# A later release for the first attention units of each head group in a two-layer hybrid decoder

## The chip, the cores and the metric

The kernel runs on one core of one Trainium2 chip. The metric is the device time of one execution in microseconds (us). Before the change it is 1654.51 us, the median of three runs that lie between 1652.82 and 1655.21 us. The engines are called PE (TensorE, with PEld for its weight loads), DVE (VectorE), ACT (ScalarE), POOL (GpSimd) and SP (SyncE, which issues every transfer of this kernel).

## The reference

The input is x, 1024 tokens by 1024 channels. Two decoder layers follow each other. In each one a token mixer is applied, then x becomes LayerNorm(alpha * x + mixer(x)), then a sigmoid gate adds a projected per-layer embedding. The mixer of the first layer, the one that matters here, is dilated sliding-window attention in three groups, (window 128, stride 1), (512, 4) and (2048, 16), with 16 heads of 64 channels each:

```python
for gi, (window, dil) in enumerate(A_GROUPS):
    q, k, v = split_cols(h[..., base:base + 3 * A_WIDTH], [A_WIDTH] * 3)   # h = x @ w_in
    q, k = apply_rope(q), apply_rope(k)
    o, lse = banded_attention(strided(q), strided(k), strided(v), window // dil)
    outs.append(o); lses.append(lse)
wts = softmax(stack(lses), axis=0)
o = einsum('gbsh,gbshd->bshd', wts, stack(outs))
return (o * silu(z)) @ w_out
```

The second layer is sliding-window attention with grouped queries and a sink logit per head.

## The kernel before, in words

Tokens are handled in 8 tiles of 128. Weights come in blocks of 1024 rows by 512 columns. A block is loaded in four pieces (`Block.load`, L102, `wraw<-in_wa_dram`), its largest entry is found on DVE (`maxima`, L109, then L226 to L230, a small matmul at L237 and L239), and it is split into a high and a low fp16 part (`split`, L132 on ACT and L133 on DVE, four pieces each). These steps form one long list, of which each projection tile draws a few (`prepare`). A raw buffer is loaded anew once its block is split, and a block is split into its slot once the block before in that slot is `released`.

A projection tile (`lin`, L272 to L274) is 24 matmuls of 512 columns on PE. The first layer (`layer_a`) goes through two halves of the heads (`pair`), each through the dilation groups 1, 2 and 0, so there are six rounds. A round has three blocks of 8 tiles, 24 tiles in all: a value block, then two query-and-key blocks (`i` = 0 and 1, four heads each, together eight heads). Two blocks of the gate z come behind the six rounds.

Behind a value tile `v_out` splits it into `vh` (L368, ACT) and `vl` (L369, DVE). Behind a query-and-key tile `rope_out` turns it: two DVE products (L347, L350), a POOL sum (L351), the high part on ACT (L357), the low part on POOL (L358), a swapped copy on ACT (L361), and one transposing transfer `qk<-hl` from SP (L362). The tile `qk` has 8 buffers.

The attention of one token tile and four heads is a unit. `score` (L385 on PE, 8 matmuls or 16 where two key tiles are seen) reads `qk`; DVE adds the mask and takes the maximum (L389, four times); ACT makes the bias (L393), four exponentials (L395) and the high part `phl` (L399); POOL, or DVE for every fourth tile, makes the low part (L401); SP transposes it to `pT` (L404). `value` (L416 to L418, 12 or 24 matmuls) multiplies by `vh` and `vl`; ACT writes it out (L695) and SP stores it (`scr<-st`, L704). In dilation group 0 the second unit of a token tile (odd `q`) hands a `merge` to a list: it loads the three dilation groups' outputs (`gt<-scr`, L752, two buffers), weighs them on DVE, ACT and POOL (L758 to L784) and stores them (`oa<-gt`, L788).

The order on PE is planned with a counter. `lin` calls `sub_tick` after the third and the sixth of its eight steps (9 and 18 matmuls), and `progress` calls it at the tile's end, so time goes in thirds of a tile:

```python
    def later(self, w, fn):
        self.due.append([self.work_done + w - 0.01, fn])

    def sub_tick(self):
        self.work_done += self.tile_w / 3.0
        ready = [e for e in self.due if e[0] <= self.work_done]
        ...
        self.credit = min(self.credit + self.upt * self.tile_w / 3.0, 2.0)
        if self.credit >= 0.999:
            self.credit -= 1.0
            self.unit_step()
```

`unit_a` is called when two thirds of its tile are counted, and asks with `later(UNIT_LAG, ...)`, UNIT_LAG = 1.67, that its unit be put at the end of the queue `self.units`. `unit_step` takes the next unit off that queue in order, runs the `value` of the unit that was taken three steps earlier, and then the `score` of the new one. `upt` is the number of steps for one tile: 0.75 in the six rounds (a step in every fourth third), 1.0 in the last block of the last round, and 2.0 from the z blocks on.

The program so written is then put in order for each engine by a scheduler that follows a modelled timeline: an instruction that the model does not see as ready is passed by later ones that are. On the chip each engine then keeps to that order.

Behind the rounds `mixed` multiplies the attention output by the gate, applies the output projection (blocks `wo`, whose memory the attention buffers held before) and normalises.

Of the kernel before, what the change touches and what calls it, by code (L numbers as in the profile page):

```python
# [78 lines left out]
UNIT_LAG = 1.67  # L79
# [60 lines left out]
class Trunk:  # L140
# [544 lines left out]
    def unit_a(self, q, g, n, qk, vh, vl, cs, ncs, cv, scr):  # L685
        nc, at = self.nc, self.att
        tiles = [n] if g == 2 or (n % 2 == 0 if g == 1 else n == 0) else [n - 1, n]
        mask = self.mask_2 if g == 2 else self.mask_a[:, (2 - len(tiles)) * P:]

        def stats():  # L690
            st = at.tile([P, 4 * HD + 8], F32, tag="st", name="st", bufs=len(self.pipe) + 1)
            return st, st[:, 4 * HD:4 * HD + 4], st[:, 4 * HD + 4:]

        def outp(o, st):
            nc.scalar.activation(st[:, 0:4 * HD], o.rearrange("p h c -> p (h c)"), AF.Copy, scale=cv)  # L695
            d = scr[q // 2][g][:, q % 2, :]
            if g == 1:
                b = 512 * (n % 2) + n // 2
                d = d[b:b + 509:4]
            elif g == 2:  # L700
                d = d[n:n + 1017:8]
            else:
                d = d[n * P:(n + 1) * P]
            nc.sync.dma_start(d, st)  # L704
            if g == 0 and q % 2:
                self.merges.append(self.merge(n, q // 2, scr[q // 2]))

        kas = [lambda h, sw, t=qk[i]: t[:, 4 + 4 * sw + h, :] for i in tiles]
        self.later(UNIT_LAG, lambda: self.unit(lambda h: qk[n][:, h, :], kas, mask, cs, ncs,
                                          lambda h, kb: vh[:, tiles[kb], h, :], lambda h, kb: vl[:, tiles[kb], h, :],  # L710
                                          stats, outp, n % 4 != 0))

# [452 lines left out]
```

## Time and profile before

| | us |
|---|---|
| median of three runs | 1654.51 |
| the profiled execution's own time | 1658.58 |
| its span, first to last instruction | 1656.8 |
| PE busy | 1584.4 (96% of the span) |
| DVE busy | 1084.4 (65%) |
| ACT busy | 922.7 (56%) |
| POOL busy | 660.2 (40%) |

The profile is of one execution, which took 4.07 us more than the median. Its mean granted TensorE clock is 0.987 of full speed. In a row of the timeline the first number is the start in us from the span's start and the second the duration; a bracket at the end gives the engine's idle time just before and what ended it. Rows that start with an engine and a line and hold "<-" are waits: total us, number, longest.

### The profile page before, as it was taken

The numbers are of one execution on the slowest core, as the hardware profiler recorded it, in microseconds if no ns is written. First come the engines' busy times: TensorE is split into PE (matmuls) and PEld (weight loads), VectorE is DVE, ScalarE is ACT, GpSimd is POOL, SyncE is SP. The second block draws the span as 40 slices with busy tenths as digits, with TensorE's granted clock in tenths as the row PEclk, the third lists the DMA queues.
The fourth block names the chain that finished last, engine by engine and source line by source line (L and its number), as shares of the span: only waits on it lengthen the run. The fifth ranks groups of instructions, "written<-read, shape, count | busy, mean of one in ns | idle before, by whom it ended". The sixth has DMA issues, their size and how long they took to land. (4 is left out here: it accounts for less than half of the span.)

```text
span 1656.8 us, 29015 instructions
## 1 busy us (share of the span) xinstructions
PE 1584.4 (96%) x10579; PEld 880.8 (53%) x10579; DVE 1084.4 (65%) x2619; ACT 922.7 (56%) x2050; POOL 660.2 (40%) x477
## 2 busy tenths in 40 slices
PE   8999999999999999989999987889999998999998
PEld 3455676655556556656545543334455555544444
DVE  6766655655666777656566657877356988778731
ACT  4537765674776576556657833533334888754321
POOL 0015624432553576345235652452323552225331
PEclk9999999999999999999999998999999999999999
DMA  9618766774886788557558986989975898998963
GB/s 362 251 61 172 174 143 139 152 166 106 167 162 177 188 208 190 153 127 167 139 130 187 194 229 212 334 208 264 242 189 107 163 204 166 197 300 212 261 197 109
DMA packets 543792, 311.02 MB, mean 188 GB/s; under 512 B 473120, under 2 KB 494240, under 8 KB 543392
## 3 DMA queue, kind: packets, MB, share of 16 engines
q1 hardware_dynamic: 543648, 309.16, 75.3%
q8 instruction: 83, 1.36, 0.3%
q14 instruction: 61, 0.50, 0.1%
HBM read 137.78 MB, written 54.92 MB: 116 GB/s over the span
## 5 line engine op out<-in xcount | busy, mean ns | idle before, releaser
L272 PE MATMUL lin<-whl,xhl 128*128 128x512 f16 x1280 | 488.6, 382 | 0.4 <-ACT zu L719 0.4
L273 PE MATMUL lin<-whl,xhl 128*128 128x512 f16 x1280 | 488.0, 381 | 0.0
L274 PE MATMUL lin<-whl,xhl 128*128 128x512 f16 x1280 | 487.7, 381 | 0.0
L351 POOL TENSOR_TENSOR t<-t,t 128x512 f32<-128x512 f32 (+1 forms) x120 | 153.9, 1282 | 303.5 <-DVE t L350 290.3
L401 POOL TENSOR_TENSOR phl<-sm,phl 128x1024 f16<-128x1024 f32 (+1 forms) x88 | 156.1, 1774 | 231.6 <-ACT phl L399 189.3
L109 DVE TENSOR_REDUCE wpm<-wraw 128x1 f32<-128x1024 f32 (+1 forms) x132 | 157.0, 1198 | 98.3 <-DMA wraw<-in_wa_dram 57.6
L274 PEld LDWEIGHTS <-xhl 128*128 128x128 f16 x1280 | 149.3, 117 | 127.7 <-issue 3.5
L272 PEld LDWEIGHTS <-xhl 128*128 128x128 f16 x1280 | 149.3, 117 | 120.1 <-issue 3.9
L273 PEld LDWEIGHTS <-xhl 128*128 128x128 f16 x1280 | 149.6, 117 | 116.7 <-issue 3.4
L395 ACT ACTIVATE sm<-sm,st,cs 128x128 f32<-128x128 f32 (+1 forms) x384 | 203.6, 532 | 3.4
L358 POOL TENSOR_TENSOR hl<-t,hl 128x512 f16<-128x512 f32 (+1 forms) x120 | 144.7, 1206 | 130.4 <-ACT hl L357 130.4
L389 DVE CUSTOM_DVE_ANT_0 sm<-s,tab 128x256 f32<-128x256 f32 (+1 forms) x512 | 157.2, 358 | 31.3 <-PE s L385 26.3
L133 DVE SCALAR_TENSOR_TENSOR whl<-wraw,s,whl 128x1024 f16<-128x1024 f32 (+1 forms) x116 | 167.3, 1492 | 10.0 <-ACT whl L132 9.9
L357 ACT ACTIVATE hl<-t 128x512 f16<-128x512 f32 (+1 forms) x120 | 72.3, 602 | 133.2 <-POOL t L351 131.4
L347 DVE TENSOR_TENSOR t<-lin,rope 128x512 f32<-128x512 f32 (+1 forms) x120 | 78.9, 657 | 77.6 <-PE lin L274 53.3
L132 ACT ACTIVATE whl<-wraw,s 128x1024 f16<-128x1024 f32 (+1 forms) x116 | 121.8, 1122 | 5.1 <-DVE s L212 5.0
L272 PE MATMUL lin<-whl,x2T 128*128 128x512 f16 (+1 forms) x320 | 114.5, 358 | 0.0
L274 PE MATMUL lin<-whl,x2T 128*128 128x512 f16 (+1 forms) x320 | 114.5, 358 | 0.0
L273 PE MATMUL lin<-whl,x2T 128*128 128x512 f16 (+1 forms) x320 | 114.5, 358 | 0.0
L399 ACT ACTIVATE phl<-sm 128x1024 f16<-128x1024 f32 (+1 forms) x128 | 110.2, 861 | 1.2
L385 PE MATMUL s<-qk 128*128 128x128 f16 x1120 | 81.7, 221 | 11.8 <-DMA qk<-hl 11.8
L361 ACT ACTIVATE hl<-hl 128x512 f16<-128x512 f16 (+1 forms) x104 | 63.2, 608 | 53.5 <-POOL hl L358 53.3
(187 smaller groups left out, 2880.9 us busy)
## 6 DMA issues: line engine op xcount, KB each, us to landing
wraw<-in_wa_dram SPq DMA_DIRECT2D x56, 512.0 KB, 5.6
scr<-st SPq DMA_DIRECT2D x96, 132.0 KB, 2.3
gt<-scr SPq DMA_DIRECT2D x48, 264.0 KB, 3.4
wraw<-in_wav_dram SPq DMA_DIRECT2D x24, 512.0 KB, 6.2
prh<-pro SPq DMA_DIRECT2D x32, 256.0 KB, 4.0
wraw<-in_wg_dram SPq DMA_DIRECT2D x16, 512.0 KB, 9.1
wraw<-in_wb_dram SPq DMA_DIRECT2D x16, 512.0 KB, 6.5
xg<-y SPq DMA_DIRECT2D x16, 512.0 KB, 3.7
```

Of the source, the lines that this page charges most:

```text
L109: k.nc.vector.tensor_reduce(pm[:, c:c + 1], self.raw[:, c * q:(c + 1) * q], axis=AX.X, op=ALU.max, apply_absolute_value=True)
L132: nc.scalar.activation(hl[:, 0, sl], self.raw[:, sl], AF.Copy, scale=self.s)
L133: self.last = nc.vector.scalar_tensor_tensor(hl[:, 1, sl], self.raw[:, sl], self.s, hl[:, 0, sl], op0=ALU.mult, op1=ALU.subtract)
L272: mm(ps, xh(kt), wh, start=(kt == 0), stop=False)
L273: mm(ps, xh(kt), wl, start=False, stop=False)
L274: mm(ps, xl(kt), wh, start=False, stop=(kt == NK - 1))
L351: self.at_pool = nc.gpsimd.tensor_add(t1[:, :nh * HD], t1[:, :nh * HD], t2[:, :nh * HD])
L358: nc.gpsimd.tensor_sub(hl[:, :nh, HD:P], rv, hl[:, :nh, 0:HD])
L389: nc.vector.tensor_tensor_reduce(sm[:, h, :nk], ps[:, i, :nk], mask, 1.0, -3e38, ALU.add, ALU.max, mx[:, h:h + 1])
L395: nc.scalar.activation(sm[:, h, :nk], sm[:, h, :nk], AF.Exp, bias=nbias[:, h:h + 1], scale=cs, accum_out=sums[:, h:h + 1])
L399: nc.scalar.activation(hl[:, 0], sm[:, :, :nk], AF.Copy)
L401: eng.tensor_sub(hl[:, 1], sm[:, :, :nk], hl[:, 0])
```

## The change

One line is added in `unit_a`, and the lag that is handed to `later` is no longer the constant. For even `q` (the block with `i` = 0 of each round) the lag of token tile n is 1.67 + max(0, 0.67 - n/3): 2.34 for n = 0, 2.00 for n = 1, and 1.67 as before from n = 2 on. For odd `q` it is 1.67 as before.

```diff
@@ -706,7 +706,8 @@
         kas = [lambda h, sw, t=qk[i]: t[:, 4 + 4 * sw + h, :] for i in tiles]
-        self.later(UNIT_LAG, lambda: self.unit(lambda h: qk[n][:, h, :], kas, mask, cs, ncs,
+        lag = UNIT_LAG + (max(0.0, 0.67 - n / 3.0) if q % 2 == 0 else 0.0)
+        self.later(lag, lambda: self.unit(lambda h: qk[n][:, h, :], kas, mask, cs, ncs,
                                           lambda h, kb: vh[:, tiles[kb], h, :], lambda h, kb: vl[:, tiles[kb], h, :],
                                           stats, outp, n % 4 != 0))
```

## Rows read from the trace of the kernel before

**Rows 1.** The page: the span and PE's share.
```profile
span 1656.8 us, 29015 instructions
PE 1584.4 (96%) x10579; PEld 880.8 (53%) x10579; DVE 1084.4 (65%) x2619; ACT 922.7 (56%) x2050; POOL 660.2 (40%) x477
```
**Rows 2.** Waits of PE, whole span: us in total, times, longest us.
```profile
PE s L237 <- DVE mdd L230: 18.7, 3, 8.0
PE s L385 <- DMA qk<-hl: 11.8, 4, 5.2
```
**Rows 3.** Timeline of PE around the first scores of rounds 2 to 5.
```profile
265.81 0.62 PE L385 MATMUL s<-qk 128*128 128x128 f16 x8 [2.46 <-DMA qk<-hl]
...
402.81 0.19 PE L416 MATMUL o<-vh,pT 128*128 128x64 f16 x1
...
407.26 0.61 PE L385 MATMUL s<-qk 128*128 128x128 f16 x8
...
550.86 0.19 PE L416 MATMUL o<-vh,pT 128*128 128x64 f16 x1
...
551.56 0.39 PE L272 MATMUL lin<-whl,xhl 128*128 128x512 f16 x1
...
554.59 0.38 PE L274 MATMUL lin<-whl,xhl 128*128 128x512 f16 x1
...
557.69 1.03 PE L385 MATMUL s<-qk 128*128 128x128 f16 x8 [2.72 <-DMA qk<-hl]
...
708.92 1.03 PE L385 MATMUL s<-qk 128*128 128x128 f16 x8 [5.18 <-DMA qk<-hl]
```
**Rows 4.** Windows behind two of them: us, busy by engine, granted PE clock, DMA.
```profile
557.69:561.00 3.31, 3.31 (x15) 1.80 (x16) 2.12 (x10) 1.17 (x3) 1.27 (x1) 0.53 1.10 357
708.92:714.50 5.58, 5.58 (x20) 2.72 (x21) 3.49 (x14) 3.58 (x11) 1.29 (x2) 0.51 0.55 134
```
**Rows 5.** Timelines of DVE, POOL and SP ahead of the 708.92 score.
```profile
693.39 5.38 DVE L133 SCALAR_TENSOR_TENSOR whl<-wraw,s,whl 128x1024 f16<-128x1024 f32 x4 [0.35 <-ACT whl L132]
698.70 0.68 DVE L347 TENSOR_TENSOR t<-lin,rope 128x512 f32<-128x512 f32 x1
...
700.05 1.28 POOL L351 TENSOR_TENSOR t<-t,t 128x512 f32<-128x512 f32 x1 [5.94 <-DVE t L350]
...
698.80 1.76 SPq L102 DMA_DIRECT2D wraw<-in_wa_dram  x4
...
703.92 2.10 SPq L362 DMA_TRANSPOSE qk<-hl  x1
```
**Rows 6.** Timelines of DVE, ACT, POOL: the round's last unit before.
```profile
686.13 0.41 DVE L389 CUSTOM_DVE_ANT_0 sm<-s,tab 128x256 f32<-128x256 f32 x1
...
687.62 0.30 ACT L393 ACTIVATE st<-mx,ncs 128x4 f32<-128x4 f32 x1 [1.25 <-DVE mx L389]
...
690.77 1.06 ACT L399 ACTIVATE phl<-sm 128x1024 f16<-128x1024 f32 x1
...
691.96 2.15 POOL L401 TENSOR_TENSOR phl<-sm,phl 128x1024 f16<-128x1024 f32 x1 [4.71 <-issue]
```
**Rows 7.** Windows ahead of the first turned tile: us, PE, PEld, DVE, ACT, POOL.
```profile
687.50:700.05 12.55, 12.55 (x90) 8.68 (x89) 9.22 (x17) 9.18 (x17) 2.15 (x1) 1.00 0.44 109
535.20:546.88 11.68, 11.68 (x97) 6.82 (x96) 10.72 (x15) 7.22 (x11) 2.25 (x3) 1.00 0.35 86
```
**Rows 8.** The layer's end: DVE's timeline, then waits of 987 to 1060 us.
```profile
938.65 0.18 DVE L758 TENSOR_REDUCE mM<-gt 128x8 f32<-128x24 f32 x1 [2.91 <-DMA gt<-scr]
...
940.34 5.77 DVE L133 SCALAR_TENSOR_TENSOR whl<-wraw,s,whl 128x1024 f16<-128x1024 f32 x4
946.02 0.17 DVE L768 TENSOR_TENSOR mwl<-mw,gt 128x24 f32<-128x24 f32 x1
...
ACT wo L132 <- DMA oa<-gt: 9.0, 1, 9.0
PE s L237 <- DVE mdd L230: 15.3, 2, 8.0
```

## The prediction

> **What bounds the kernel now.** The page comes first: PE is busy for 96% of the span [rows 1], so only PE's own waits, or stretches in which it runs slowly, are there to be won. The list of PE's waits comes next. Its largest entry is outside the attention rounds (the matmul of L237, 18.7 us); the second is scores that wait for `qk<-hl`, 11.8 us in four waits [rows 2]. The timeline of PE shows where three of them are: at 265.81, 557.69 and 708.92 us, after waits of 2.46, 2.72 and 5.18 us, 10.36 us together [rows 3]. Each is the first score (n = 0, `i` = 0) of a round: of rounds 2, 4 and 5. Such a score is asked for 1.67 tiles behind its projection tile, while the transfer that it reads is issued only after DVE, POOL and ACT have turned the tile. The chain ahead of the worst one [rows 5] shows why that is late: the weight split holds DVE for 5.38 us before L347 at 698.70, the POOL sum follows at 700.05, and the transfer is issued at 703.92, behind four weight loads, to land 5 us later.
>
> The waits cost more than their length. In the windows behind the second and the third the granted clock is 0.53 and 0.51 of full speed [rows 4], that is 1.2 GHz and not 2.4. PE works all through them, so (1 - 0.53) x 3.31 = 1.6 us and (1 - 0.51) x 5.58 = 2.7 us are lost, 4.3 us in all. Behind the wait of 2.46 us the matmul's duration is the usual one of full clock, 0.62 us beside 0.61 in round 3 and 1.03 in rounds 4 and 5 [rows 3].
>
> **The change, part by part.** I count in thirds of a tile, from the start of a round of 24 tiles. `unit_a` is called for tile 8 + n at third 26 + 3n. A lag of 1.67 makes the unit available at third 31 + 3n. A step comes at every fourth third: 32, 36, 40 and so on. So now unit n of the round's sixteen is taken at 32 + 4n: arrivals are 3 apart and steps 4 apart, and the queue only grows. With the change unit 0 arrives at 33 and unit 1 at 35 (a lag of 2.34 or 2.00, less 0.01, rounded up to a third). The step at 32 finds nothing new, unit 0 is taken at 36, unit 1 at 40, and unit n at 36 + 4n. **All sixteen units of each round move one step back**, not two of them, as the queue is taken in order. The two steps a round without a new unit, now at thirds 96 and 100, become 100 and 104. No instruction is added or removed; PE, the other engines and SP do the same work in another order.
>
> What is moved, and what it passes:
>
> 1. The first score goes back by four thirds, which are 9 + 6 + 9 + 6 = 30 projection matmuls in the place where it stood. One is 0.216 us: 14 steps from 551.56 to 554.59 [rows 3]. That is 6.5 us. The `value` that stood one step earlier (the round's last unit) now comes directly before it: 24 matmuls, 0.70 us from 550.86 to 551.56 [rows 3]. Without the wait PE would thus reach the first score at 265.81 - 2.46 + 6.5 + 0.7 = 270.6 in round 2, against a landing at 265.81: 4.7 us to spare. In round 5 it is 708.92 - 5.18 + 7.2 = 710.9: 2.0 to spare, or 1.7, as the value that stays ahead is one of 12 matmuls and not of 24 (0.35 us). In round 4 the scheduler had already let 15 matmuls pass (551.56 to 554.59), so only 15 more come in between: 557.69 - 2.72 + 3.25 + 0.7 = 558.9, 1.2 us to spare. If landings stay where they are, all three waits and both slow stretches go: -10.4 - 4.3 = **-14.7 us**.
>
> 2. The landings need not stay. The round's last unit, whose softmax now runs before the first turned tile, comes one step nearer to it. Ahead of round 5 it takes four maxima on DVE from 686.13 (0.34 apart, 1.4 us), 4.2 us of ACT from 687.62 to 691.83, one other copy included, and 2.15 us of POOL [rows 6]. If nothing of it finds room, the landing is 1.4 + 4.2 + 2.15 = 7.75 us later; if its old place is used by the weight split instead, the landing is earlier by up to those 1.4 us of DVE. The engines do have room: ahead of round 5's first turned tile DVE is busy 9.22 of 12.55 us, ACT 9.18, POOL 2.15; ahead of round 4's, DVE 10.72 of 11.68, ACT 7.22, POOL 2.25 [rows 7]. Only round 4's DVE is nearly full, by 1.4 us of new work against 1.0 of idle time. I take 1 us of new waits, nearer the low bound, since the rows show idle time on all three engines; the bounds are 0 and all that point 1 gains. SP's queue gets one `pT` transfer nearer to the four weight loads; its issue is like the 2.10 us of L362 [rows 5], and its landing is needed twelve thirds later.
>
> 3. Buffers: `qk` tile n of the second block is written at third 50 + 3n or later, its last reader, unit n + 1, is taken at 40 + 4n: 64 against 68 at n = 6, and there the turning still comes in between. `vh` is written from third 74 on, tile 0 first; the last value of the first block is at 76 instead of 72 and reads tiles 6 and 7. I cost both at nothing.
>
> 4. The layer's end. From the second-last block's end upt rises to 1.0 and then 2.0, so the delay shrinks to a third, but one more unit falls among the z tiles, and the merges of the last round begin one step, one tile, later: 24 x 0.216 + 0.7 + 1.2 (twice the 0.62 of a score of 8 matmuls [rows 3]) = 7.1 us. This matters: `wo` cannot be split before the last `oa<-gt` has landed (ACT waits 9.0 us for it), and PE's matmul of L237 waits 15.3 us there, in two waits, for what follows on DVE [rows 8]. But the first merge, loaded at 938.65, gets on only at 946.02, after 5.77 us of weight split [rows 8]. A start 7.1 us later, 945.8, still meets that. So most is absorbed, and what is left is the extra unit's DVE and POOL work, 1.4 to 3.6 us. I take +2; bounds 0 and +7.1.
>
> Sum: -14.7 + 1 + 2 = -11.7 us on the profiled execution's 1658.58, so 1646.9; the median lies 4.07 lower: **1642.8 us**.
>
> **The rivals.** *Partly handed back.* The merges keep their whole 7.1 us, and rounds 4 and 5 wait for some 2 us in all: -14.7 + 7.1 + 2 = -5.6, about 1648.9. For it speaks that ACT's 9.0 us and PE's 15.3 us [rows 8] hang on the last merge; against it the 7.4 us between 938.65 and 946.02.
>
> *The wait only moves.* If the landings follow by 4.8 us, the three scores wait 0.1, 3.6 and 3.1 us, and those of rounds 3 and 6, which go 11 matmuls and a value later than now (3.1 us), up to 1.7 each: 10.2 us, as much as now, and the slow clock stays: no change, 1654.5. The same comes out if the lag is not what orders PE, since the scheduler already holds back scores that its model sees as late (19 matmuls in round 3: 407.26 - 402.81 less 0.35, by 0.216 [rows 3]). Against it: the 708.92 score was not held back at all.
>
> *Slower: the last unit's softmax stands in front of the first turned tile.* Place: the DVE, ACT and POOL queues at the start of rounds 2 to 6. At the full 7.75 us the waits are 3.0, 6.5 and 6.0, and up to 4.6 each in rounds 3 and 6: 24.7 against 10.4, so +14.3; it decides from about 5 us of delay. At 6 us, 1.3 + 4.8 + 4.3 + 2.9 + 2.9 = 16.2 us of waits and 2 of the layer's end give +7.8, 1662. Against it stands the idle time of [rows 7].
>
> The Trainium skill (Perfetto Trace Analysis, section on the Tensor Engine instruction) says that ACT, DVE and GPSIMD are strict FIFO. By that alone whatever is put ahead of L347 delays it, and the sum would be this rival's 1669 and not 1643. The trace agrees on the order, for L347 starts at 698.70 as the four splits end; it does not show that the added pieces must all fall ahead of it.
>
> **How the numbers follow.** Forecast 0.60, partly handed back 0.18, the wait only moves 0.10, slower 0.12. A measurement of this kernel can tell some 0.2%, 3.3 us, from no change. The first two cases are faster by more: 0.78; the third is the same: 0.10; slower 0.12. The range: at its low end the full 14.7 and the fourth wait for qk, 11.8 - 10.4 = 1.4 [rows 2], with as much again for the clock, 1637; at its high end it takes in the handed-back case and most of the third, 1655. It leaves out the slower case and little more.
>
> **What would show it.** Right: no bracket `<-DMA qk<-hl` over 2 us at the first scores of rounds 2, 4 and 5, full clock behind them, and those scores exactly 72 matmuls behind their tile. Step 2 is wrong if L362 of a round's first tile is issued later against the tile's end than now; step 4 if `ACT wo <- DMA oa<-gt` or the L237 waits grow. The forecast fails if these waits grow by as much as the scores lose.

## The result: slower by 1.3%, and the profile after

The changed kernel takes **1676.93 us** (median of four runs, 1672.14 to 1682.10), the kernel before 1654.86 in the same session (four runs, 1652.82 to 1657.38). The ratio is 1.0133 with a 95% interval of 1.0099 to 1.0167. Forecast were 1642.8 us and a range that ends at 1655: wrong, and on the other side. The profiled execution of the changed kernel took 1678.25 us, 19.7 more than that of the kernel before.

The page, answering to [rows 1]:

```profile
span 1676.5 us, 29005 instructions
...
PE 1599.1 (95%) x10579; PEld 886.7 (53%) x10579; DVE 1088.9 (65%) x2619; ACT 921.0 (55%) x2050; POOL 660.3 (39%) x477
```

The span grew by 19.7 us. PE ran the same 10579 matmuls, but was busy for 14.7 us longer (1584.4 to 1599.1) and idle for 5.0 longer (72.4 to 77.4). So most of the loss in this pair of profiles is not waiting but matmuls that run slowly. Where it lies is shown by two windows of each, cut where tile 160 starts, that is where the first layer's attention and gate are done and its output projection begins (length, PE busy, granted clock, DMA share, GB/s; first before, then changed):

```profile
0.00:1052.46 1052.46, 1009.48 (x6850) 0.98 0.72 177
1052.46:1656.80 604.34, 574.87 (x3729) 0.99 0.82 206
...
0.00:1066.35 1066.35, 1016.02 (x6849) 0.98 0.70 175
1066.35:1676.50 610.15, 583.06 (x3730) 0.97 0.82 204
```

Up to there the changed kernel is 13.9 us behind, 6.5 of it in longer busy time and 7.4 in waits. The other 8.2 us of busy time, and 5.8 us of the loss, come later, behind the part of the program that the change touches.

The waits of PE over the whole span (us in total, times, longest) show what PE waits for in the changed kernel, and the last row what the first of them was before:

```profile
PE o L416 <- ACT st L695: 23.8, 9, 5.3
PE o L416 <- DMA pT<-phl: 9.6, 9, 2.4
PE lin L272 <- ACT whl L132: 8.4, 1, 8.4
PE s L237 <- DVE mdd L230: 7.9, 2, 4.5
PE s L385 <- DMA qk<-hl: 1.6, 2, 1.0
...
PE o L416 <- ACT st L695: 2.7, 2, 2.0
```

Against [rows 2], `qk<-hl` fell from 11.8 to 1.6, as forecast. In its place stands an entry that was 2.7 us in two waits before: the first matmul of a `value` (L416) waits for the write-out of values on ACT (L695). PE's timeline shows the first scores of rounds 2, 4 and 5, which answer to [rows 3], and four of the nine waits for the write-out:

```profile
269.16 0.61 PE L385 MATMUL s<-qk 128*128 128x128 f16 x8
...
566.16 0.23 PE L385 MATMUL s<-qk 128*128 128x128 f16 x1 [1.03 <-DMA qk<-hl]
...
724.97 0.23 PE L385 MATMUL s<-qk 128*128 128x128 f16 x1 [0.59 <-DMA qk<-hl]
...
348.25 0.19 PE L416 MATMUL o<-vh,pT 128*128 128x64 f16 x1 [2.29 <-ACT st L695]
...
495.50 0.21 PE L416 MATMUL o<-vh,pT 128*128 128x64 f16 x1 [2.68 <-ACT st L695]
...
658.22 0.21 PE L416 MATMUL o<-vh,pT 128*128 128x64 f16 x1 [5.28 <-ACT st L695]
...
998.71 0.21 PE L416 MATMUL o<-vh,pT 128*128 128x64 f16 x1 [4.64 <-ACT st L695]
```

The first three waits for ACT lie at the starts of rounds 3, 4 and 5 (tiles 49, 73 and 97), the fourth in the z tiles. The windows behind three of them (length, PE busy, granted clock, DMA share, GB/s) show the price of each beyond its length:

```profile
348.25:352.00 3.75, 3.75 (x23) 0.54 0.40 112
658.22:665.00 6.78, 6.78 (x46) 0.68 0.59 182
998.70:1003.00 4.30, 4.29 (x32) 0.50 0.66 220
```

PE is busy throughout at some half to two thirds of its full clock, as it was behind the waits of [rows 4]. In the rounds the slow stretches have moved with the waits, and there are more of them.

Why is the write-out late? At the start of round 5 the value to be written out ends on PE at 644.69:

```profile
644.50 0.19 PE L418 MATMUL o<-vh,pT 128*128 128x64 f16 x1
```

ACT's timeline from there, first the changed kernel, then the same place in the kernel before:

```profile
648.12 0.63 ACT L361 ACTIVATE hl<-hl 128x512 f16<-128x512 f16 x1 [1.38 <-POOL hl L358]
648.65 0.61 ACT L399 ACTIVATE phl<-sm 128x512 f16<-128x512 f32 x1
650.59 0.63 ACT L357 ACTIVATE hl<-t 128x512 f16<-128x512 f32 x1 [1.32 <-POOL t L351]
653.02 0.63 ACT L361 ACTIVATE hl<-hl 128x512 f16<-128x512 f16 x1 [1.80 <-POOL hl L358]
653.56 4.25 ACT L132 ACTIVATE whl<-wraw,s 128x1024 f16<-128x1024 f32 x4
657.71 0.45 ACT L695 ACTIVATE st<-o,cv 128x256 f32<-128x256 f32 x1
```

```profile
641.21 0.61 ACT L357 ACTIVATE hl<-t 128x512 f16<-128x512 f32 x1
641.72 4.26 ACT L132 ACTIVATE whl<-wraw,s 128x1024 f16<-128x1024 f32 x4
645.89 0.46 ACT L695 ACTIVATE st<-o,cv 128x256 f32<-128x256 f32 x1
...
646.39 0.19 PE L416 MATMUL o<-vh,pT 128*128 128x64 f16 x1 [2.00 <-ACT st L695]
```

In both, four pieces of the weight split (4.25 us) stand ahead of the write-out. In the changed kernel copies of turned tiles that wait for POOL (1.38, 1.32 and 1.80 us) stand there too. The write-out begins 13.0 us after its value's end, and 0.51 us later PE goes on with the next value. Before, it began 9.25 us after its value's end (636.64), and PE waited 2.00 us.

ACT's timeline has the same picture at six of the nine waits, 16.5 of the 23.8 us: the four split pieces stand directly ahead of the write-out. At the wait of 4.64 us in the z tiles they do not. There ACT first stands still for a merge:

```profile
998.08 0.22 ACT L764 ACTIVATE mw<-mw 128x24 f32<-128x24 f32 x1 [9.96 <-DVE mw L760]
```

### The profile page after: what moved, and what is told of

Its sections match the earlier page's. It is cut to its first block, busy times and chain, and to the rows that moved or that the text cites. A ratio compares the mean times of both kernels' runs of the same rounds, so it can differ in the third digit from the quotient of the medians.

```text
span 1676.5 us, 29005 instructions
## 1 busy us (share of the span) xinstructions
PE 1599.1 (95%) x10579; PEld 886.7 (53%) x10579; DVE 1088.9 (65%) x2619; ACT 921.0 (55%) x2050; POOL 660.3 (39%) x477
## 4 chain that ended last, share of the span: by engine, by line
PE 26%; DVE 9%; DMA 7%; issue 7%; POOL 5%; ACT 4%; SPq 2%; POOLq 0%; DVEq 0%; ACTq 0%
PE lin L272 8%; PE lin L273 8%; PE lin L274 8%; DVE whl L133 2%; POOL hl L358 2%; ACT sm L395 2%; POOL t L351 2%; POOL phl L401 1%; DVE sm L389 1%; DMA wraw<-in_bo_dram 1%; DVE wpm L109 1%; ACT whl L132 1%; DMA og<-za 1%; POOL og L920 1%; DMA wraw<-in_wb_dram 1%
## 5 line engine op out<-in xcount | busy, mean ns | idle before, releaser
L133 DVE SCALAR_TENSOR_TENSOR whl<-wraw,s,whl 128x1024 f16<-128x1024 f32 (+1 forms) x116 | 166.0, 1479 | 8.8 <-ACT whl L132 8.8
L347 DVE TENSOR_TENSOR t<-lin,rope 128x512 f32<-128x512 f32 (+1 forms) x120 | 78.7, 656 | 50.4 <-PE lin L274 29.6
L417 PEld LDWEIGHTS <-pT 128*128 128x128 f16 x800 | 72.7, 99 | 43.1 <-issue 33.7
```

Of the source, the lines that this page charges most:

```text
L133: self.last = nc.vector.scalar_tensor_tensor(hl[:, 1, sl], self.raw[:, sl], self.s, hl[:, 0, sl], op0=ALU.mult, op1=ALU.subtract)
```

## The experiments

Times are medians; ratios are to the kernel before, run beside each. Where the text speaks of tiles, it compares when PE starts the first matmul of a projection tile (24 matmuls each, counted through the program; rounds start at tiles 0, 24, 48, 72, 96 and 120, z at 144). From the PE timelines, us later (+) or earlier (-) than in the kernel before:

| tile | changed | `hold` | `hold_before` | `score_both` | `catch_up` |
|---|---|---|---|---|---|
| 24 | -1.7 | -3.5 | -2.5 | -0.6 | +0.6 |
| 40 | -3.9 | -5.8 | -5.1 | -3.2 | -2.8 |
| 72 | -0.6 | -6.6 | -5.1 | -3.2 | +4.3 |
| 88 | +2.6 | -9.4 | -7.6 | -6.0 | +0.5 |
| 104 | +13.5 | -0.7 | -7.5 | -6.3 | +7.2 |
| 108 | +6.9 | -8.0 | -15.5 | -14.3 | -0.8 |
| 144 | +9.7 | -10.3 | -15.0 | -13.1 | +9.4 |
| 160 | +13.9 | -6.1 | -17.3 | -16.0 | +6.6 |
| 264 | +19.7 | -7.7 | -18.3 | -18.3 | +11.0 |

Each column is a single execution; that of the kernel before (1658.58) lies 3 to 6 us above its medians, so a column's end is that much too low against the runs; `hold`'s own is 3.9 us under its median, `catch_up`'s 4.4 above.

**Theory 1**: the queue's step back lets the last units of a round fall behind the weight split and the turned tiles in ACT's queue, and PE then waits for their write-outs. **Rival**: the loss is something else that the later units bring, most of all the merges at the layer's end.

### ACT's order mended: `hold`

The changed kernel, with each ACT piece of the split issued behind the latest write-out:

```diff
-            nc.scalar.activation(hl[:, 0, sl], self.raw[:, sl], AF.Copy, scale=self.s)
+            with k.tc.issue_after(k.at_evac.ins) if k.at_evac else nullcontext():
+                nc.scalar.activation(hl[:, 0, sl], self.raw[:, sl], AF.Copy, scale=self.s)
...
-            nc.scalar.activation(st[:, 0:4 * HD], o.rearrange("p h c -> p (h c)"), AF.Copy, scale=cv)
+            self.at_evac = nc.scalar.activation(st[:, 0:4 * HD], o.rearrange("p h c -> p (h c)"), AF.Copy, scale=cv)
```

> The changed kernel, with each ACT piece of the weight split ordered behind the last write-out of a value (L695). Theory 1: the five waits of PE for ACT st L695 in the rounds (2.3, 2.7, 2.8, 1.6 and 5.3 us in the changed kernel) and the slow clock behind them, some 18 us in all, come from four split pieces that stand in ACT's queue ahead of the write-out of the value at the block's start. Then these waits are under 1 us here, tile 144 starts some 18 us earlier than in the changed kernel, and the time is 1656 to 1662 us. Rival: the waits come from the softmax of the round's last unit in front of the first turned tile, or from the backlog of POOL; then the order of the split does not matter, the waits stay above 2 us, and the time is 1672 to 1680 us.

Measured 1654.9 us (10 runs), ratio 0.9998 [0.998, 1.0015]: the whole loss of 22 us is gone. PE's waits (the edit adds a line or two, so L695 is L697 here):

```profile
PE lin L274 <- DVE wpm L109: 17.3, 1, 17.3
...
PE o L418 <- ACT st L697: 2.2, 2, 1.1
```

The waits for the write-out fell from 23.8 to 2.2. ACT now takes the split in parts, with a write-out ahead of each; one such place:

```profile
645.98 0.46 ACT L697 ACTIVATE st<-o,cv 128x256 f32<-128x256 f32 x1
646.34 2.18 ACT L133 ACTIVATE whl<-wraw,s 128x1024 f16<-128x1024 f32 x2
```

Theory 1 has the place and the sign; the gain is larger than it said (1656 to 1662 us), and the two waits that are left are 1.1 us each and not under 1. DVE's pieces of the split (L133 in the kernel before) need ACT's, so they move with them: the run shows what the place of the split is worth, not ACT's part of it alone. And the waits for `qk` had been won already in the changed kernel, so more than a return to the old time should have been in reach.

### The last round: `not_last` and `last_only`

The shift without the last round, and the shift in the last round alone:

```diff
-        lag = UNIT_LAG + (max(0.0, 0.67 - n / 3.0) if q % 2 == 0 else 0.0)
+        lag = UNIT_LAG + (max(0.0, 0.67 - n / 3.0) if q % 2 == 0 and (q, g) != (2, 0) else 0.0)   # not_last
+        lag = UNIT_LAG + (max(0.0, 0.67 - n / 3.0) if (q, g) == (2, 0) else 0.0)                  # last_only
```

> The changed kernel, with the later release left out in the last round only (second half of the heads, dilation group 0). Theory 1: what the changed kernel loses from tile 136 on (6.3 us behind at tile 136, 19.7 at the end, so 13 us) is due to the last round's shift alone, which puts one more unit among the z tiles and starts the merges later; then 1662 to 1666 us, with rounds 1 to 5 as in the changed kernel. Rival: it follows from the whole kernel being out of step, and stays; 1674 to 1679 us.

> The kernel before, with the later release in the last round only. Theory 1: rounds 1 to 5 as before, with the three waits for qk of 2.5, 2.7 and 5.2 us, and some 11 to 13 us more from tile 136 on: 1665 to 1668 us. Rival (the end's loss comes from the shift of the earlier rounds): 1653 to 1657 us.

Measured 1666.75 us, ratio 1.0074 [1.0051, 1.0098], and 1667.16 us, ratio 1.008 [1.0054, 1.0106]: the last round costs some 13 us, the other five some 12 together, and the two make 25 where the whole change costs 22. `last_only` lies within its expectation, `not_last` 0.75 us above its own. In `last_only` PE's longest waits between 920 and 1060 us are:

```profile
PE lin L272 <- ACT whl L132: 8.5, 1, 8.5
PE s L237 <- DVE mdd L230: 7.2, 1, 7.2
PE o L416 <- ACT st L695: 5.8, 3, 3.0
```

Of the two waits at L237 [rows 8, 15.3 us] one is left. In the place of the other, at tile 160, PE waits 8.5 us for the split, and the 5.8 us of waits for write-outs are new. The profiled executions of `last_only` and of the kernel before differ by 5.2 us in span only, so most of the 13 us cannot be placed in this pair. The changed kernel against `not_last` places them better, as only the last round differs: `not_last` is later than the kernel before by 8.9 us at tile 144, 6.6 at 160 and 7.0 at 264, the changed kernel by 9.7, 13.9 and 19.7. So, in single executions, the last round's loss arises from the z tiles on, and about half of it behind tile 160. The rival has a part in it: the layer's end is half of the loss, and one of the write-outs there stands behind a merge (998.08 in the changed kernel).

### The first score alone: `score_late` and `score_later`

The kernel before, its queue untouched, with the first unit's score alone put 1.0 or 1.33 tiles later:

```diff
         if new:
-            new["score"]()
+            if new["late"]:
+                self.later(new["late"], new["score"])
+            else:
+                new["score"]()
...
-                                          stats, outp, n % 4 != 0))
+                                          stats, outp, n % 4 != 0, late=1.0 if q % 2 == 0 and n == 0 else 0.0))   # 1.33 in score_later
```

> The kernel before, with the score of each round's first unit (even q, n = 0) put one tile later, while the queue of units keeps its steps. Theory 1: the shift of the fifteen other units is what costs, and the later first score is what gains; here the waits for qk at the first scores of rounds 2, 4 and 5 go, nothing else moves, and the time is 1640 to 1648 us. Rival: any later score of the first unit brings the waits for the write-out, because the units bunch up; 1655 us or more.

> The kernel before, with the first score of each pair of groups alone put 1.33 tiles later, the queue of units as it was (score_late had 1.0, with 8.4 us of waits for qk left, 3.4 the longest). Theory 1 (those waits and the slow clock behind them are what can be won, and the queue's step back is what costs): the waits fall under 4 us, and the time to 1641 to 1647. Rival (what is left hangs on the landings, which follow the score, or a score so close to the next one makes DVE and ACT late): 1648 to 1656.

Measured 1648.64 us, ratio 0.997 [0.9954, 0.9986], and 1650.27 us, ratio 0.9975 [0.996, 0.999]. Both gain a little, and both less than theory 1 expected (`score_late` by 0.6 us); `score_later` falls into the rival's range, with waits for `qk` of still 7.6 us. PE's timeline in round 5 of `score_later` shows whose they are:

```profile
710.06 0.61 PE L388 MATMUL s<-qk 128*128 128x128 f16 x8
...
713.91 0.29 PE L388 MATMUL s<-qk 128*128 128x128 f16 x2 [3.24 <-DMA qk<-hl]
```

The first unit's score runs at 710.06 without a wait; the second unit's, directly behind it, waits 3.24 us. The first two tiles of a round are late; as long as the first waited, its wait hid the second's.

### The first two scores: `score_both`

```diff
+                                          stats, outp, n % 4 != 0, late=(1.33, 1.0)[n] if q % 2 == 0 and n < 2 else 0.0))
```

> The kernel before, the queue of units as it was, with the first score of each pair of groups put 1.33 tiles later and the second 1.0 later. In score_later the waits for qk that are left (3.10 and 3.24 us) are those of the second unit's score, whose tile is as late as the first's. Theory (the first two tiles of a round are late, and the queue need not step back for them): these two waits and the slow clock behind them go as well, waits for qk under 3 us, 1641 to 1646. Rival (the third unit's score then waits, or the probabilities of the first two come late for their values): qk or pT waits take their place, 1648 to 1655.

Measured **1641.91 us** (6 runs), ratio 0.9917 [0.9895, 0.9938], faster than either kernel. PE is busy 4.9 us less than in [rows 1] with the same matmuls (from the page), and waits 2.9 us for write-outs and 2.0 for `qk` (from its waits):

```profile
PE 1579.5 (96%) x10579; PEld 880.5 (54%) x10579; DVE 1076.6 (66%) x2619; ACT 919.1 (56%) x2050; POOL 664.5 (41%) x477
```

```profile
PE o L419 <- ACT st L698: 2.9, 2, 2.0
PE s L388 <- DMA qk<-hl: 2.0, 2, 1.4
```

This kernel puts the first two scores about where the change puts them, and leaves the other units. So the difference between the two, 1676.9 against 1641.9 in different sessions, **some 35 us, is the price of the queue's step back**. What the change wins and what it loses are now apart.

### Is ACT's order worth something by itself: `hold_before` and `both_hold`

The edit of `hold`, on the kernel before and on `score_both`.

> The kernel before, with the weight split's pieces on ACT issued after the latest write-out of values, as in hold, and no shift of the units. Theory 1 (the shift lets the write-out of values fall behind the split pieces, and that is its whole loss): before has only 2.7 us of values waiting for a write-out, so the order is worth little without the shift, 1649 to 1655. Rival (the order of the split is a gain of its own, and hold merely adds it to the loss of the shift): it gains as much here as it did on the changed kernel, 22 us, so 1630 to 1638.

> score_both with the weight split's pieces on ACT behind the latest write-out, as in hold_before. Theory (both remove the same waits, those of a round's first scores; hold by earlier landings, score_both by later scores): the gains don't add, 1638 to 1645. Rival (they are two gains of 12 us each): 1626 to 1633.

Measured 1643.01 us, ratio 0.9929 [0.9908, 0.995], and 1641.55 us, ratio 0.9924 [0.9906, 0.9943]. `hold_before` lies between the two expectations: 12.7 us of gain, not 0 to 6 and not 22. Its waits for `qk` are 2.2 us in place of 11.8 [rows 2]. The new order brings the landings forward, by way of DVE: in the kernel before four pieces of the split on DVE stand ahead of the first product (L347) of round 5's first turned tile [rows 5], while in `hold_before` only one piece does. Counted from the end of that projection tile, the product begins 2.4 us later in place of 5.3, and the transfer is issued 7.8 us later in place of 10.5 (the tile ends at 685.89 here, at 693.40 before):

```profile
688.26 0.68 DVE L349 TENSOR_TENSOR t<-lin,rope 128x512 f32<-128x512 f32 x1
...
693.69 1.42 SPq L364 DMA_TRANSPOSE qk<-hl  x1
```

With `score_both` the new order adds nothing: both remove the same waits. So `hold` must be read against `hold_before`, where the waits for `qk` are won as well: under the mended order the step back costs 0.7% (0.9998 against 0.9929), 11 us, and under the old one 35. **Some 24 of the 35 us hang on the place of the split in the order**, 11 do not; the four intervals leave the 24 open by some 8 us either way.

### The PSUM tile: `s_three` and `o_two`

The two slots of values share one PSUM tile, and a value waits for the write-out of the value before it, though that lies in the other slot. `o_two` gives each slot a tile of its own; the bank for it is taken from the scores, and `s_three` is the control for that. Both start from the changed kernel:

```diff
-        self.ps_s = ec(tc.tile_pool(name="ps_s", bufs=4, space=PSUM))
+        self.ps_s = ec(tc.tile_pool(name="ps_s", bufs=3, space=PSUM))        # s_three and o_two
-        self.o_ps = self.ps_o.tile([P, 2, 4, HD], F32, tag="o", name="o")
+        self.o_ps = [self.ps_o.tile([P, 4, HD], F32, tag="o%d" % i, name="o") for i in range(2)]   # o_two
```

> The changed kernel with three instead of four PSUM tiles for scores and maxima: the control for o_two, which has to take a bank from somewhere. Both theories: the scores' softmax may wait for a free tile now and then; 1674 to 1684 (the changed kernel: 1677), and values that wait for their predecessor's write-out stay at 18 to 28 us.

> As s_three, with the two result slots of the values in two PSUM tiles of a bank each, and not in one tile. Theory 1 (a value waits because it shares a PSUM tile with the value before it, whose write-out is late): the next value may start while the write-out is still queued, so the waits of L416 for ACT fall from 23.8 to under 5 us, and the time is 13 to 22 us under s_three. Rival (the late write-out holds up what comes behind it in another way, the store, the merges or the softmax in ACT's queue): within 5 us of s_three, with other waits in place of these.

Measured 1687.19 us, ratio 1.019 [1.0167, 1.0212], and 1694.02 us, ratio 1.0232 [1.0212, 1.0253]. Theory 1 as it stood in these expectations fell. `s_three` is 3 us slower than both theories allowed, and `o_two`, 6.8 us slower than `s_three`, has the rival's sign but lies outside its 5 us. PE's waits, first `s_three`, then `o_two`:

```profile
PE o L416 <- ACT st L695: 17.8, 9, 3.4
...
PE s L385 <- DVE mx L389: 9.0, 11, 1.8
...
PE o L416 <- DMA pT<-phl: 7.1, 7, 1.8
```

```profile
PE o L416 <- DMA pT<-phl: 23.0, 17, 3.9
PE s L385 <- DVE mx L389: 20.1, 12, 3.9
```

With two tiles the waits for the write-out are gone (17.8 to none in the list), and 15.9 us of waits for the probabilities and 11.1 for the maxima stand in their place. At tile 144 `o_two` is 1.7 us behind `s_three`; the rest of the 6.8 arises later. So the shared tile is where PE was stopped, and freeing it won nothing. That takes back theory 1's second half (the tile). It fits the first (ACT's order), if ACT's queue is late with everything that the last units need, write-outs and probabilities alike; that the split causes the new waits was not tried.

### The rest under the mended order: `hold_not_last`

> hold with the shift left out of the layer's last round. Theory 1b (with ACT's order mended, the 12 us by which hold still lies above hold_before are two separate losses: some 8 us at tiles 88 to 104, some 6 us at the layer's end behind the merges): the end's part goes, 1647 to 1651. Rival (the end only passes on what the rounds lose, or what the last round loses comes back elsewhere): as hold, 1653 to 1657.

Measured 1652.45 us, ratio 0.9982 [0.9965, 1.0]. That lies between the two expectations and cannot be told from `hold` (0.9998 [0.998, 1.0015]): of the 11 us that the step back still costs under `hold`, the last round has 2.5 by the medians, and most must lie elsewhere. The table has two places. At tiles 88 to 104 `hold` loses 8.7 us, where `hold_before` loses 0.1 (`hold_not_last` loses 7.6 there). From 144 to 160 `hold` loses 4.2, where `hold_before` wins 2.3: PE waits 17.3 us at tile 160 (its longest wait, shown above), where it waits 8.9 us in `hold_not_last`. The timelines of DVE and ACT in `hold` show what is late in the first place:

```profile
658.95 0.18 DVE L761 TENSOR_REDUCE mM<-gt 128x8 f32<-128x24 f32 x1 [5.39 <-DMA gt<-scr]
...
660.78 0.30 ACT L395 ACTIVATE st<-mx,ncs 128x4 f32<-128x4 f32 x1 [5.65 <-DVE mx L391]
```

DVE stands 5.39 us at a merge whose load has not landed, with the maxima of a unit queued behind it, and ACT waits 5.65 us for those. That this is the cause was not tried.

### The last units back in their places: `catch_up`

The changed kernel with one more step of the queue at unit 8 of each round, so that units 10 to 15 are taken where they were before:

```diff
+        if q % 2 and n == 5:
+            self.later(0.33, self.extra_step)
...
+    def extra_step(self):
+        self.credit += 1.0
```

> The changed kernel with one more step of the queue in each round, at its unit 8 (third 66), so that units 10 to 15 are taken where they were before and only units 0 to 9 go later. Theory (the step back costs by the round's last units, which then fall beside the next round's first turned tiles and its weight split): most of the 35 us between the changed kernel and score_both comes back, the values' waits for ACT fall under 6 us, waits for qk stay under 4, 1640 to 1648. Rival (what costs is the step back of the units inside the round, whose values and transfers lose their slack, and the place of the last units matters little): 1662 to 1677.

Measured 1665.25 us, ratio 1.0065 [1.0048, 1.0081]: a third of the 35 us only, within the rival's range; the waits for the write-out did not fall under the 6 us of the theory. PE's waits:

```profile
PE o L419 <- DMA pT<-phl: 18.6, 13, 3.5
...
PE o L419 <- ACT st L698: 9.8, 11, 1.8
```

Waits for the write-out fell from 23.8 to 9.8, and those for `pT` doubled from 9.6 to 18.6. From tile 72 to 88, with the last units in their old places, it wins 3.8 us on the kernel before, where the change loses 3.2; but it loses 3.8 us more between tiles 40 and 72 and 7.4 more between 108 and 144, where the extra step puts two units two thirds of a tile apart (some of both is only a unit's matmuls on the other side of a boundary). So the experiment paid part of its own price, and how the 35 us divide between the last units and the others stays open.

## Why the prediction was wrong

**What bounds the kernel** was read rightly: the late first scores and the slow clock behind them. `score_both`, which removes little else, wins 2.6 us between tiles 24 and 40, 2.8 between 72 and 88, and 8.0 between 104 and 108: 13.4 us against the 14.7 of the forecast, and 11.9 in the runs.

**Point 1** held in the changed kernel itself: waits for `qk` of 11.8 us became 1.6, and the first scores of rounds 2, 4 and 5 stand where the reckoning in thirds put them, exactly 72 matmuls behind their tiles, with full clock behind them. All that was to show this point right came, and the kernel was slower. It missed that the second tile is as late as the first; the change moves that one too, so it cost nothing.

**Point 2**, +1 us for later landings, measured 1.6 us (1.03 and 0.59), near by luck: the sign that it named for being wrong came. Counted from the end of the first turned tile, its transfer was issued at 10.0, 16.5 and 14.4 us in rounds 2, 4 and 5, where it had been 6.0, 9.6 and 10.5, and it landed 2.0, 3.9 and 2.6 us later than before. The later scores had just the slack to take most of that in, and in round 4 PE had already lost 1.44 us to a wait for `pT` ahead of the score. Between 2.3 and 2.8 us of the delay are SP's: the tile was ready, and the `pT` transfer of the last unit stood in front. In round 5:

```profile
716.65 4.46 SPq L404 DMA_TRANSPOSE pT<-phl  x1
721.20 1.47 SPq L362 DMA_TRANSPOSE qk<-hl  x1
```

The prediction gave the issue of that transfer 2.10 us; it took 4.0, 6.5 and 4.5. The point also asked only what the last unit's softmax does to the first turned tile, and not what the turned tiles and the weight split do to the last unit. Of `pT` it said that its landing is needed twelve thirds later, and took that as slack.

**Point 3 is the step that failed**: "I cost both at nothing". It named the buffers of `qk` and `vh`, and left out the PSUM tile of the values and the write-out (L695) behind which it comes free. Before, a write-out was late already at the same place: it stood behind 4.26 us of split (641.72), and PE waited 2.00 us for it. One step later in the round copies that wait for POOL came ahead of it as well, and 2.7 us of waits became 23.8, with the clock at 0.50 to 0.68 behind the longer ones. Of PE's 14.7 us of longer busy time 6.5 lie up to tile 160, and those include these stretches. The cause was shown, for some 24 of the 35 us, by `hold` against `hold_before`: with the split's pieces in another place of the order the step back costs 11 us and not 35. What the 11 are made of stays open. The Trainium skill (PSUM — Partial Sum Buffer, section on PSUM bank collisions) has a rule that bears on the place: PSUM is to be guarded by bank and not by address, since two engines at different columns of one bank, on the same partitions, collide all the same. Under that rule two slots in one bank serve as one buffer. The waits in the rows above agree, and `o_two` ended them; but it made nothing faster, so here the rule tells where PE stops and not what the time would be.

**Point 4**, +2 us with 7.1 as its bound, was mis-sized: `last_only` measured 13 us. Neither sign that it named came: in the changed kernel ACT's wait for `oa<-gt` fell from 9.0 to 4.0 us, and in `last_only` the wait at L237 from 15.3 to 7.2. What was not weighed is ACT's queue there: 5.8 us of waits for write-outs (8.2 in the changed kernel, the 4.64 us behind a merge among them), the 8.5 us for the split in place of the second L237 wait, and the loss behind tile 160. With `hold`'s order the last round's shift costs 2.5 us by the medians (`hold_not_last`), which cannot be told from nothing; so most of this, too, hangs on that order.

**The rivals.** "Slower" had the sign, at 0.12, and the queues at the starts of rounds as its place, but not the way: no wait for `qk` grew. Its mechanism was there in part, since landings came 2.0 to 3.9 us later, under the 5 us or so from which it was to decide; but in rounds 2 and 5 most of the later issue arose in SP's queue, which it did not name. The Trainium skill's sentence (Perfetto Trace Analysis, Tensor Engine Instruction) that ACT, DVE and GPSIMD are strict FIFO would have given 1669; measured were 1677, but not by the waits for `qk` that the 1669 adds up, so that it lies near is chance. The rows agree with the rule, and with a use of it that the prediction did not make: what stands at the head of the queue delays the last unit's own results. "Partly handed back" and "the wait only moves" did not come, though in `score_later` the wait did move, to the second unit.

## What to carry to other kernels

A queue that is taken in order moves as a whole: for its last elements, list every engine's queue in which they now stand, and every result of theirs that PE needs before it can go on, the write-out that frees PSUM among them. Where only the first consumers are late, move these and not the queue: that was worth 35 us here against moving the queue, and 12 against the kernel before. And look at the order on the engine that turns, splits and writes out before giving any consumer more slack; yielding four long weight pieces to a short write-out was worth as much as the best move of the scores (12.7 us against 11.9), and the two did not add up.

## What the runs showed that was not expected

More idle time can cost less than slow time: `catch_up` leaves PE idle for 80.7 us (1667.8 less 1587.1) against 77.4 in the changed kernel, and is faster since PE is busy 12 us less; its mean granted clock is 0.986 against 0.978. Its waits for write-outs are 11 of at most 1.8 us, and the changed kernel's 9 of up to 5.3, with the granted clock at 0.50 to 0.68 behind the longer ones. And one bank fewer for the scores alone cost 10 us (1676.9 to 1687.2), with 9.0 us of waits of L385 for maxima where the changed kernel had 0.3. But at tile 144 `s_three` is only 1.2 us behind the changed kernel, at 160 5.1 and at 264 9.9, so most of the cost arises behind the rounds, and its cause was not tried.
